# Eight of 22 up-projection steps as seven block products each, with the operand sums on GpSimd

## The chip, the cores and the metric

One Trainium2 chip, one of its cores. The metric is the device time of one execution in microseconds; the time of a kernel is the median of its runs.

## The reference, cut to what matters

One layer of a diffusion backbone over 512 latent tokens of width 1024, with 256 context tokens. A token mixer (a two-way state-space scan beside windowed attention) comes first. Its output is added to the stream, and then the part that the change touches follows, the gated feed-forward block:

```python
D_MODEL = 1024; SEQ = 512; D_FF = 2816

def conv_ffn(h, w_up, conv_w, conv_b, w_down):
    u = dwconv_centred(h @ w_up, conv_w, conv_b)     # 3 taps along the tokens
    a, b = u[..., :D_FF], u[..., D_FF:]
    return (jax.nn.silu(a) * b) @ w_down

x = x + gt1 * o_lat
x = x + gt2 * conv_ffn(modulate(x, norm2_g, sh2, sc2), w_up, ffn_conv_w, ffn_conv_b, w_down)
return rmsnorm(x, final_g)
```

All tensors are fp32.

## The kernel before

Every fp32 product is made as three products of a split operand. ScalarE rounds an operand to its high part (`hi`), VectorE subtracts to get the low part (`lo`), and TensorE adds up hi x hi, hi x lo and lo x hi in one PSUM bank. `split` (L180 to L182) does this for a piece of weights of 128 x 1024; `gemm` (L224 to L234) issues the matmuls, eight blocks of 128 of the inner dimension with three matmuls each, 512 tokens wide.

The program is a list of steps, each with the keys of the weights it needs. `run` walks the list and calls `load` for the weights one key ahead of the step that uses them; a load is a DMA on the SP queue into one of three `wraw` buffers and a split into one of two pairs of buffers `whi` and `wlo`. The order of each engine is then set by a scheduler that goes by readiness and by program order among what is ready. It is written out by hand only inside `manual_schedule`, and instructions given to `keep_in_program_order` keep their order among themselves.

The **up projection** has 22 steps (`up_step(t)`, NFF = 22). A step multiplies the normed input `h2h`, `h2l` (the high and low parts, tokens along the free dimension) with two weight pieces of 128 columns each: key `("up", t)` for the half called a, `("up", 22 + t)` for the half called b. Each half is one bank `pa` or `pb` of 512 tokens, 24 matmuls. `up_first` makes the convolution of a (a copy with scale on ScalarE, two multiply-adds on VectorE that read PSUM), a tanh, and the silu; `up_second` does the convolution of b and multiplies. The product goes to `F["x"][t % 2][:, t // 2]`. Step 0 is special: its matmuls are 256 wide, by halves of the tokens, since the input's norm is finished beside it (L1920). Eight pieces of the modulation vector (`m_step`, multiply-adds at L787 and L789) and eight transposes of the stream (`x1_turn`, L1950) are woven between the steps.

The **down projection** is already made as seven block products (`down_step(j, u)`, j = 0 to 6): the operand `F["x"]` is taken as four blocks, by the parity of t and by the halves of the tokens (`HALF`), called e, f, g and h in the code; the sums of weight blocks were formed in DRAM by accumulating DMAs, queued on GpSimd early in the program. The sums of operands are formed by `f_sums` at the end of each up step on VectorE, and `f_split` splits an operand of the next product into `F["s"]`, either there (for products 0 and 1) or during the product ahead. `near_last` and `near_out` finish the last rows after the last matmul.

There are eight PSUM banks, three under the name `acc` and five under `mis`. GpSimd does nothing in up steps 1 to 21.

## Time and profile before

| | us |
|---|---|
| median of 3 runs | 1225.29 |
| lowest and highest run | 1224.85, 1225.33 |
| the profiled execution, its own time | 1223.88 |
| its span | 1222.1 |
| TensorE busy | 1210.9 |
| VectorE busy | 919.6 |
| ScalarE busy | 682.7 |
| GpSimd busy | 196.2 |

The up projection lies at about 863 to 1107 us of the span and the down projection at 1107 to 1213. In the profile PE is TensorE's matmuls, PEld its weight loads, DVE is VectorE, ACT ScalarE, POOL GpSimd and SP the queue that issues most DMAs. A matmul's listed duration includes time in which the next one already runs, so busy PE time says only that it did not stop. A row of a group gives line, engine, operation, output and inputs, shapes and count, then busy time and mean duration in ns, then the engine's idle time just before and what ended it. A row of the timeline gives the start, the duration, and the instruction.

### The profile page before, as it was taken

How to read it: one execution, taken by the hardware profiler on the slowest of the kernel's cores; microseconds unless marked ns; L12 is line 12 of the kernel's file. 1: busy time of each engine (PE TensorE's matmuls, PEld its weight loads, DVE VectorE, ACT ScalarE, POOL GpSimd, SP SyncE). 2: the span in 40 equal slices, each digit the busy share in tenths (PEclk: the TensorE clock that was granted, in tenths of full speed). 3: DMA queues.
4: the chain of work that ended last, by engine and by line, in shares of the span. 5: the costliest groups of instructions: out<-in, count | busy, mean ns of one | idle time of the engine just before them, and what ended most of it. 6: DMA issues, size and time to landing. Idle time of an engine off the chain costs nothing.

```text
span 1222.1 us, 17422 instructions
## 1 busy us (share of the span) xinstructions
PE 1210.9 (99%) x6310; PEld 994.8 (81%) x6310; DVE 919.6 (75%) x1481; ACT 682.7 (56%) x1275; POOL 196.2 (16%) x187
## 2 busy tenths in 40 slices
PE   9999999999999999999999999999999999999996
PEld 6798888888878877778777778888988888888885
DVE  5857888888654598697896868577787777777786
ACT  5658788787444467486575663223543434335653
POOL 0000121101000043352451631000200000000053
PEclk9999999999999999999999999999999999999999
DMA  9645789844754435346365568777266533347852
GB/s 372 255 137 183 160 252 256 173 153 125 174 160 151 129 104 176 109 133 195 102 176 194 159 214 273 230 249 224 56 149 162 167 107 103 120 125 181 290 162 87
DMA packets 122551, 211.55 MB, mean 173 GB/s; under 512 B 26720, under 2 KB 69024, under 8 KB 122464
## 3 DMA queue, kind: packets, MB, share of 16 engines
q1 hardware_dynamic: 111280, 186.83, 48.8%
q0 software_dynamic: 10752, 23.07, 8.5%
q8 instruction: 50, 0.82, 0.3%
q10 hardware_dynamic: 432, 0.53, 0.1%
q14 instruction: 37, 0.30, 0.1%
HBM read 185.68 MB, written 42.28 MB: 187 GB/s over the span
## 4 chain that ended last, share of the span: by engine, by line
PE 95%; ACT 1%; DVE 1%; POOL 1%; issue 1%; DMA 0%; POOLq 0%; DVEq 0%; ACTq 0%
PE acc L231 20%; PE acc L234 20%; PE acc L232 20%; PE score L951 3%; PE po L1000 3%; PE pt L987 2%; PE mis L573 2%; PE mis L1604 2%; PE mis L1497 2%; PE mis L2102 1%; PE mis L2100 1%; PE mis L2101 1%; PE mis L1612 1%; PE acc L1070 1%; PE acc L1072 1%; PE acc L1071 1%
## 5 line engine op out<-in xcount | busy, mean ns | idle before, releaser
L181 ACT CAST whi<-wraw 128x1024 fp32r<-128x1024 f32 (+1 forms) x115 | 120.3, 1047 | 157.4 <-PE acc L232 113.3
L231 PE MATMUL acc<-hlh,whi 128*128 128x512 f32 x472 | 194.1, 411 | 0.0
L182 DVE TENSOR_TENSOR wlo<-wraw,whi 128x1024 fp32r<-128x1024 f32 (+1 forms) x115 | 144.1, 1253 | 64.4 <-ACT whi L181 61.0
L232 PE MATMUL acc<-hll,whi 128*128 128x512 f32 x472 | 185.0, 392 | 0.0
L234 PE MATMUL acc<-hlh,wlo 128*128 128x512 f32 x472 | 185.0, 392 | 0.0
L231 PE MATMUL acc<-mh,whi 128*128 128x512 f32 x368 | 143.4, 390 | 0.0
L232 PE MATMUL acc<-ml,whi 128*128 128x512 f32 x368 | 143.2, 389 | 0.0
L234 PE MATMUL acc<-mh,wlo 128*128 128x512 f32 x368 | 143.2, 389 | 0.0
L234 PEld LDWEIGHTS acc<-hlh,wlo 128*128 128x128 f32 x472 | 88.6, 188 | 19.5
L231 PEld LDWEIGHTS acc<-hlh,whi 128*128 128x128 f32 x472 | 88.8, 188 | 17.9 <-issue 3.1
L232 PEld LDWEIGHTS acc<-hll,whi 128*128 128x128 f32 x472 | 88.9, 188 | 17.4 <-issue 2.4
L234 PEld LDWEIGHTS acc<-mh,wlo 128*128 128x128 f32 x368 | 69.1, 188 | 14.5
L231 PEld LDWEIGHTS acc<-mh,whi 128*128 128x128 f32 x368 | 69.1, 188 | 14.3
L232 PEld LDWEIGHTS acc<-ml,whi 128*128 128x128 f32 x368 | 69.1, 188 | 14.1
L1385 DVE SCALAR_TENSOR_TENSOR ta<-acc,half,ta 128x511 f32<-128x511 f32 (+1 forms) x66 | 43.9, 665 | 26.4 <-ACT ta L1384 26.0
L960 DVE CUSTOM_DVE_ANT_0 p<-score,winm,nsink 128x512 f32<-128x512 f32 (+1 forms) x64 | 51.9, 810 | 15.3 <-PE score L951 13.8
L1384 ACT ACTIVATE ta<-acc,half 128x512 f32<-128x512 f32 (+1 forms) x66 | 46.8, 709 | 22.8 <-PE acc L234 21.6
L967 ACT ACTIVATE p<-p,mneg 128x512 f32<-128x512 f32 (+1 forms) x64 | 49.7, 778 | 15.4 <-DVE mneg L960 14.8
L162 POOL DMA_DIRECT2D dsum<-wdn x24 | 25.4, 1143 | 193.0 <-DVE wlo L1084 171.7
L1499 POOL TENSOR_TENSOR st<-st,eT 128x512 f32<-128x512 f32 x24 | 29.7, 1239 | 165.4 <-ACT st L1516 152.0
L231 PE MATMUL acc<-hch,whi 128*128 128x256 f32 x176 | 54.7, 311 | 0.0
L995 DVE TENSOR_TENSOR ptl<-pt,pth 128x512 fp32r<-128x512 f32 x72 | 47.5, 685 | 8.5 <-ACT pth L991 7.9
(426 smaller groups left out, 2998.7 us busy)
## 6 DMA issues: line engine op xcount, KB each, us to landing
wraw<-wup SPq DMA_DIRECT2D x44, 512.0 KB, 3.6
dsum<-wdn POOLq DMA_DIRECT2D x24, 704.0 KB, 9.0
fb<-cs_d SPq DMA_DIRECT2D x32, 512.0 KB, 6.3
wraw<-wm SPq DMA_DIRECT2D x32, 512.0 KB, 3.7
wraw<-wx SPq DMA_DIRECT2D x24, 512.0 KB, 3.5
wm<-wm SPq DMA_DIRECT2D x16, 512.0 KB, 8.0
wraw<-wz SPq DMA_DIRECT2D x16, 512.0 KB, 3.6
wraw<-wos SPq DMA_DIRECT2D x16, 512.0 KB, 4.6
```

The costliest lines, as they stand in the source:

```text
L181: S.copy(hi[:, :n], r[:, :n])
L182: return V.tensor_tensor(lo[:, :n], r[:, :n], raw(hi[:, :n]), ALU.subtract)
L231: T.matmul(ps, wh, xh[:, k0 + k, :], start=a, stop=False)
L232: T.matmul(ps, wh, xl[:, k0 + k, :], start=False, stop=False)
L234: T.matmul(ps, wl, xh[:, k0 + k, :], start=False, stop=b)
L951: T.matmul(ps[:, o : o + len(z) * P], Q[h][:, b * P : (b + 1) * P], k[:, j, z[0] * P : (z[-1] + 1) * P], start=v == 0 and o % 512 in (0, P ...
L960: V.tensor_tensor_reduce(p[:, :w], d["ps"][i][:, o0 : o0 + w], m, op0=ALU.add, op1=ALU.min, scale=1.0, scalar=nsink[:, h : h + 1], accum_o ...
L967: S.activation(p, p, AF.Exp, bias=d["mneg"][:, i : i + 1], scale=-1.0, accum_out=d["den"][:, i : i + 1])
L995: V.tensor_tensor(d["ptl"][x], d["pt"][x], raw(d["pth"][x]), ALU.subtract)
L1000: T.matmul(d["po"], vst[:, cols[x], j, :], d[y][x], start=x == 0 and y == "pth", stop=x == c - 1 and y == "ptl")
L1384: S.activation(o[:, :n], ps[:, :n], AF.Identity, scale=hcol(base_w, stride + i), bias=hcol(base_b, i))
L1385: V.scalar_tensor_tensor(o[:, 1:n], ps[:, 0 : n - 1], hcol(base_w, i), o[:, 1:n], ALU.mult, ALU.add)
```

## The change

Steps 5, 7, ... 19 of the up projection (`W_STEPS`) are made by `w_step` in place of `up_step`. The two weight pieces of a step (a above b, each with two halves of 512 of the inner dimension) and the input (two halves of the inner dimension, two of the tokens) are taken as 2 x 2 blocks, and the result is formed from seven products of blocks in place of eight. A product has four blocks of the inner dimension with three matmuls each, 256 tokens wide (`w_product`).

- Of the seven weight operands three are blocks as they are (two in `uA`, one in `uD`) and four are sums. `w_prepare`, called two steps ahead, loads the pieces with three DMAs and makes the sums with four 512-wide operations on GpSimd. `w_split` splits the sums into `F["wx"]`, two before the new step (in the ordinary step ahead of it) and two in it; `uA` and `uD` are split by `load` into the usual buffers.
- Four sums of input blocks are made once, in steps 0 to 2 (`h_work`, `h_sum`), on VectorE and GpSimd, and split into `F["hs"]`.
- In a new step three products are copied from PSUM by ScalarE, GpSimd adds three times 256 columns, and VectorE makes four 256-wide sums that write PSUM. Then the old `up_first` and `up_second` follow. The product of a and b is made on GpSimd in these steps.
- The operand sums of the down projection are no longer made in the up steps by VectorE (`f_sums` is gone) but in products 0 to 2 by GpSimd (`f_sum`). One operand is split with a changed sign. Product 1's operand is split during product 0. The operand tiles take the space of the new step's tiles once step 19 is over.
- The finish of the last rows changes its order: `near_last` is called by halves, and the roots come after.
- `x1_turn` uses another temporary, and the transposes and the row loads stand four places earlier among the steps.
- GpSimd's instructions of this whole last part of the program keep program order.

```diff
@@ load
+        if key[0] in ("uA", "uD"):
+            hi, lo = (wpool.tile([P, 1024], F32R, tag=x, name=x, bufs=2) for x in ("whi", "wlo"))
+            r = F["wr"][:, :1024] if key[0] == "uA" else F["wr"][:, 1024:]
+            split(r, r.shape[-1], hi, lo)
+            return hi, lo
@@ close_c1, up_second
-    def f_sums(t):
-        p, (x, y) = t // 2, F["x"]
-        e, f, g, h = (a[:, p, z] for a in (x, y) for z in HALF)
-        one = slice(p, p + 1)
-        if t % 2 == 0:
-            f_split(0, one, x[:, one, HALF[0]])
-            V.tensor_tensor(e, e, f, ALU.subtract)
-            f_split(1, one, x[:, one, HALF[0]])
+    FS = [slice(3 * i, min(3 * i + 3, DK)) for i in range(4)]
+    def f_sum(j, z):
+        e, f, g, h = (F["x"][i][:, z, HALF[u]] for i in range(2) for u in range(2))
+        t = F["t"][:, z, :]
+        if j == 1:
+            G.tensor_tensor(t, e, f, ALU.subtract)
+        elif j == 2:
+            G.tensor_tensor(t, t, h, ALU.add)
+        elif j == 4:
+            G.tensor_tensor(f, h, f, ALU.subtract)
+        else:
+            G.tensor_tensor(t, t, g, ALU.subtract)
...
-        V.tensor_tensor(F["x"][t % 2][:, t // 2, :], a, b, ALU.mult)
-        f_sums(t)
+        (G if t in W_STEPS else V).tensor_tensor(F["x"][t % 2][:, t // 2, :], a, b, ALU.mult)
...
+    W_STEPS = range(5, 20, 2)
+    def h_sum(i, u=None):
+        (eh, el), (fh, fl), (gh, gl), (hh, hl) = ([raw(x) for x in h_parts(i)] for i in range(4))
+        x, z = F["wr"][:, :1024].rearrange("p (k t) -> p k t", k=4), slice(0, 4)
+        if i == 0:
+            V.tensor_tensor(x, fh, eh, ALU.subtract)
+            V.tensor_tensor(x, x, fl, ALU.add)
+            V.tensor_tensor(x, x, el, ALU.subtract)
+        elif i == 2:
+            x, z = tmp("te").rearrange("p (k t) -> p k t", k=2), slice(2 * u, 2 * u + 2)
+            G.tensor_tensor(x, hh[:, z], fh[:, z], ALU.subtract)
...
+    def h_work(t):
+        if t == 0:
+            h_split(0, h_sum(0))
+            F["h"] = [h_sum(2, 0), h_sum(1), h_sum(2, 1)]
+        elif t == 1:
+            h_split(1, F["h"][1])
+            h_split(2, F["h"][0])
+            F["h"].append(h_sum(3))
+        elif t == 2:
+            h_split(3, F["h"][3])
+            h_split(2, F["h"][2])
...
+    def w_prepare(t):
...
+        nc.sync.dma_start(wr[:, :1024], top)
+        nc.sync.dma_start(s[0], low[:, :512])
+        nc.sync.dma_start(wr[:, 1024:], low[:, 512:])
...
+        G.tensor_tensor(s[2], a, s[0], ALU.subtract)
+        G.tensor_tensor(s[0], s[0], d, ALU.add)
+        G.tensor_tensor(s[1], s[0], a, ALU.subtract)
+        G.tensor_tensor(s[3], b, s[1], ALU.subtract)
+    def w_split(i):
+        hi, lo = (F["wx"][:, i, u, :] for u in range(2))
+        for u, r in enumerate((F["ws"][1 + i], F["ws"][3 * i])):
+            z = slice(512 * u, 512 * u + 512)
+            pin(S.copy(hi[:, z], r), V.tensor_tensor(lo[:, z], r, raw(hi[:, z]), ALU.subtract))
+    def w_step(t):
+        def fn(wa, wd):
+            b1, b3, b2, b5, b4 = accb(), accb(), misb(), misb(), misb()
+            w_split(1)
...
+            w_product(b1, wa, 0, e, True)
+            S.copy(p1, b1[:, :HL])
+            w_product(b2, wb, 0, t2, True)
+            S.copy(p6, b2[:, :HL])
+            G.tensor_tensor(p6, p1, p6, ALU.add)
+            w_product(b3, wd, 0, t4, True)
+            w_product(b1, wa, 1, g, False)
...
+            V.tensor_tensor(x, b3[:, :HL], p6, ALU.add)
+            w_product(b5, wc, 0, t3, True)
+            V.tensor_tensor(b3[:, :HL], b5[:, :HL], x, ALU.add)
+            w_product(b4, wb, 1, t1, True)
+            S.copy(p5, b4[:, :HL])
+            G.tensor_tensor(p1, p1, p5, ALU.add)
+            G.tensor_tensor(p5, p6, p5, ALU.add)
+            w_product(b2, wc, 1, h, False)
+            V.tensor_tensor(b1[:, HL:], b2[:, :HL], p1, ALU.add)
+            V.tensor_tensor(b3[:, HL:], b5[:, :HL], p5, ALU.add)
+            if t + 2 in W_STEPS:
+                w_prepare(t + 2)
+            a = up_first(b1, b3, t)
+            up_second(a, b3, t)
+        return [("uA", t), ("uD", t)], fn
@@ up_step
                 a = up_first(pa, pb, t)
+                if t + 1 in W_STEPS:
+                    w_split(0)
                 gemm([(pb, h2h, h2l)], wb)
             up_second(a, pb, t)
+            if t < 3:
+                h_work(t)
+            elif t == 20:
+                operand_tiles()
+            if t + 2 in W_STEPS:
+                w_prepare(t + 2)
+            if t > 19:
+                f_split(0, slice(0, 6) if t == 20 else slice(6, DK), F["x"][0][:, slice(0, 6) if t == 20 else slice(6, DK), HALF[0]])
@@ x1_turn
-            t = tmp("te")
+            t = hpool.tile([P, L], F32, tag="q2", name="xo")
@@ down_step
-                    for f in (near_last, near_out):
-                        for i in TWO:
-                            f(i)
+                    near_last(0, 0), near_last(0, 1)
+                    near_last(1, 0), near_root(0), near_last(1, 1), near_root(1)
+                    near_out(0), near_out(1)
...
+            if j == 0 and u == 0:
+                for z in FS:
+                    f_sum(1, z)
+            v = u - (j < 2)
+            if j < 6 and 0 <= v < 4:
+                z = FS[v]
+                f_split((j + 1) % 2, z, OPERAND[j + 1]()[:, z, :], j == 1)
+                if j in (0, 1, 2):
+                    f_sum((2, 6, 4)[j], z)
@@ the list of steps
-        + weave(weave([up_step(t) for t in range(NFF)], msteps[24:]), [([], lambda: None)] * 6 + [x1_turn(c) for c in range(8)] + [x1_rows] + [([], lambda: None)] * 7)
+        + weave(weave([(w_step if t in W_STEPS else up_step)(t) for t in range(NFF)], msteps[24:]), [([], lambda: None)] * 2 + [x1_turn(c) for c in range(8)] + [x1_rows] + [([], lambda: None)] * 11)
...
+    with tc.manual_schedule(engines={mybir.EngineType.Pool}):
+        run(prog, early=("g", 15))
```

More of the change, by code (lines that the diff above doesn't have):

```diff
@@ new lines, in w_split, with w_product @@
+    def w_split(i):
[3 more added lines that the diff above has]
+            pin(S.copy(hi[:, z], r), V.tensor_tensor(lo[:, z], r, raw(hi[:, z]), ALU.subtract))
+    def w_product(bank, w, u, x, first):
+        (wh, wl), (xh, xl) = w, x
+        with tc.manual_schedule(engines={mybir.EngineType.PE}):
+            for k in range(4):
+                c = slice(512 * u + k * P, 512 * u + k * P + P)
+                T.matmul(bank[:, :HL], wh[:, c], xh[:, k, :], start=first and k == 0, stop=False, skip_group_check=True)
+                T.matmul(bank[:, :HL], wh[:, c], xl[:, k, :], start=False, stop=False, skip_group_check=True)
+                T.matmul(bank[:, :HL], wl[:, c], xh[:, k, :], start=False, stop=k == 3, skip_group_check=True)
```

80 lines of the change are left out of this document (56 added, 24 removed).

## The prediction

> **What bounds the kernel now.** I read the page's head, its clock row and its chain of waits first.
>
> ```profile
> span 1222.1 us, 17422 instructions
> PE 1210.9 (99%) x6310; PEld 994.8 (81%) x6310; DVE 919.6 (75%) x1481; ACT 682.7 (56%) x1275; POOL 196.2 (16%) x187
> PEclk9999999999999999999999999999999999999999
> PE 95%; ACT 1%; DVE 1%; POOL 1%; issue 1%; DMA 0%; POOLq 0%; DVEq 0%; ACTq 0%
> ```
>
> TensorE carries 95% of the chain at an undiminished clock, so only fewer or shorter matmuls can gain, and any wait put into the matmul stream is paid in full. Then busy times by stretch: steps 1 to 21 of the up projection, one crowded stretch of the scan for comparison, and the first block of the down projection.
>
> ```profile
> 877.90:1107.00 229.10, 229.10 (x1017) 189.69 (x1016) 178.58 (x258) 94.89 (x130) 0.00 (x0) 1.00 0.44 131
> 600.00:640.00 40.00, 40.00 (x245) 31.39 (x244) 37.43 (x55) 31.46 (x79) 22.71 (x21) 1.00 0.55 164
> 1107.00:1122.00 15.00, 15.00 (x69) 12.41 (x68) 10.68 (x16) 7.58 (x10) 0.00 (x0) 1.00 0.99 187
> ```
>
> The columns are length, then PE, PEld, DVE, ACT, POOL, clock, DMA. In the 229.1 us of the 21 steps TensorE never stops, VectorE works 178.58, ScalarE 94.89 and GpSimd nothing.
>
> A listed matmul duration includes pipelining, so the price of one is the distance between starts, from the timeline: 512 columns wide in the up projection, then 256 columns wide just before it, with two weight loads of that stretch.
>
> ```profile
> 949.77 0.39 PE L231 MATMUL acc<-mh,whi 128*128 128x512 f32 x1
> ...
> 953.85 0.39 PE L231 MATMUL acc<-mh,whi 128*128 128x512 f32 x1
> ```
>
> ```profile
> 862.00 0.28 PE L1775 MATMUL acc<-mh,wlast 128*128 128x256 f32 x1
> ...
> 864.88 0.28 PE L1920 MATMUL acc<-ml,whi 128*128 128x256 f32 x1
> ```
>
> ```profile
> 862.12 0.19 PEld L1774 LDWEIGHTS acc<-ml,wlast 128*128 128x128 f32 x1
> 862.24 0.19 PEld L1775 LDWEIGHTS acc<-mh,wlast 128*128 128x128 f32 x1
> ```
>
> Eighteen spacings lie between the first two rows: 4.08 / 18 = 0.2267 us. Twenty-four between the next two: 2.88 / 24 = 0.120 us. The 0.19 us loads start every 0.12 us, so at 256 columns they still overlap.
>
> **TensorE's part.** A step has 2 x 8 x 3 = 48 matmuls of 512: 10.88 us. (21 of them make 228.5, and the stretch has 229.1.) A block-product step has 7 x 4 x 3 = 84 matmuls of 256: 10.08 us. Each of the eight replaced steps therefore saves 0.80, together **-6.4 us**. The margin is narrow: a spacing of 10.88 / 84 = 0.1295 would undo it. I take 0.120, because L1775 and L1920 load a new weight for each matmul as the new products do.
>
> The Trainium skill speaks against this: "TensorE: Matmul & The Clock Gate", section Back-to-back issue gap, gives sustained spacings of about 81 ns at 128 columns and 131 ns at 512. A line between them puts 256 at 98 ns, an estimate from that page by which a new step would cost 84 x 98 = 8.2 us against 48 x 131 = 6.3, 1.9 more. The trace does not agree: 227 ns at 512 and 120 ns at 256, so here the spacing follows the columns.
>
> **VectorE's part.** Rows for what is added and removed:
>
> ```profile
> 1115.37 1.23 DVE L182 TENSOR_TENSOR wlo<-wraw,whi 128x1024 fp32r<-128x1024 f32 x1
> 1116.52 0.69 DVE L182 TENSOR_TENSOR wlo<-dnraw,whi 128x512 fp32r<-128x512 f32 x1
> L1881 DVE SCALAR_TENSOR_TENSOR fx<-fx,fx 128x256 f32<-128x256 f32 x11 | 4.7, 424 | 0.3
> L1902 DVE TENSOR_TENSOR fx<-ta,tc 128x512 f32<-128x512 f32 x22 | 15.2, 690 | 0.6
> L1852 DVE SCALAR_TENSOR_TENSOR tb<-x,a,mis 128x256 f32<-128x256 f32 x16 | 6.9, 475 | 1.7 <-PE mis L293 1.5
> L789 DVE SCALAR_TENSOR_TENSOR tm<-wraw,csil,tm 128x512 f32<-128x512 f32 x42 | 32.3, 769 | 5.4 <-DMA wraw<-wm 4.6
> L181 ACT CAST whi<-dnraw 128x512 fp32r<-128x512 f32 x4 | 2.5, 614 | 0.3 <-PE mis L2101 0.3
> ```
>
> Back to back, each starts about 0.09 before the one ahead ends (1115.37 to 1116.52 is 1.15): 1.15 for a 1024-wide split, 0.60 for 512, 0.33 for a sum of 256 columns in SBUF, 0.40 with a PSUM operand. Two steps, an ordinary one and a new one, now take 2 x 178.58 / 21 = 17.0 of 21.76 us. Removed: six operand splits and sums per pair (2.0) and the new step's product of a and b (0.6, to GpSimd). Added: the seven weight operands need a 1024-wide split and five of 512 (4.15) where there were two of 1024 (2.3), so +1.85; four PSUM sums, +1.6. New need: **17.85 of 20.96 us**. ScalarE goes from 2 x 94.89 / 21 = 9.0 to about 11.5 (three more 512 copies, three 256 copies), far from binding.
>
> **GpSimd's part, and the port.** It gets, per pair, four 512-wide weight sums and the product of a and b, and three 256-wide sums. The nearest rows:
>
> ```profile
> L1617 POOL TENSOR_TENSOR dx<-dx,te 128x512 f32<-128x512 f32 x16 | 25.1, 1566 | 1.1
> L1857 POOL TENSOR_TENSOR ml<-ta,mh 128x256 fp32r<-128x256 f32 x8 | 5.9, 735 | 11.9 <-ACT ta L1856 11.9
> ```
>
> That is 5 x 1.57 + 3 x 0.74 = 10.0 us per pair, beside 20.96, and its results are wanted about half a step later or more. GpSimd itself is no bound. But the crowded stretch shows what it does to VectorE:
>
> ```profile
> 617.37 1.30 POOL L1615 TENSOR_TENSOR dx<-dx,te 128x512 f32<-128x512 f32 x1 [3.91 <-DVE te L1606]
> 618.74 2.16 POOL L1617 TENSOR_TENSOR dx<-dx,te 128x512 f32<-128x512 f32 x1
> ```
>
> ```profile
> 605.53 1.79 DVE L1393 SCALAR_TENSOR_TENSOR CT<-tb,ta 128x512 f32<-128x512 f32 x1
> 617.53 2.21 DVE L182 TENSOR_TENSOR wlo<-wraw,whi 128x1024 fp32r<-128x1024 f32 x1
> 619.67 1.51 DVE L1393 SCALAR_TENSOR_TENSOR tc<-tb,ta 128x256 f32<-128x256 f32 x1
> 627.59 1.19 DVE L1393 SCALAR_TENSOR_TENSOR tc<-tb,ta 128x512 f32<-128x512 f32 x1 [0.40 <-ACT tb L1392]
> 632.72 1.21 DVE L1393 SCALAR_TENSOR_TENSOR tc<-tb,ta 128x256 f32<-128x256 f32 x1
> 634.06 1.57 DVE L789 SCALAR_TENSOR_TENSOR tm<-wraw,csil,tm 128x512 f32<-128x512 f32 x1
> L1393 DVE SCALAR_TENSOR_TENSOR tc<-tb,ta x36: 405/692/1519, 377.0 to 656.3; 128x256 f32<-128x256 f32 x20, 128x512 f32<-128x512 f32 x16
> ```
>
> They take turns. The split started at 617.53 lasts 2.21 instead of 1.23: it runs only once GpSimd's sum has ended at 618.67. GpSimd's next sum then waits for it, and the operation of 619.67 waits for that. All stretched rows read two SBUF operands; each lasts 0.5 to 1.1 above its usual (1.23; 0.69 and 0.41 from L1393; 0.77). The six add 1.10 + 0.98 + 1.10 + 0.50 + 0.80 + 0.80 = 5.3 us to VectorE, for 22.71 us of GpSimd: 0.23 per us. The Trainium skill says in "GPSIMD Engine Reference", section Key points, only that both share their SBUF interfaces and contend when VectorE reads two SBUF inputs; the turns are the trace's. At 0.23, the new pair adds 2.3: **20.2 of 20.96**. The stretch at 600 has VectorE at 37.43 of 40 with TensorE unbroken, so 96% need not cost anything.
>
> What costs is the tightest deadline. In a new step the 512-wide operand "uD" takes the weight buffer freed when the step before ends, and is wanted by product three: its low part at 2 x 1.44 + 0.24 = 3.12 us after the start. Copy 0.61 and split 0.69 leave 1.8 of cover. Steps 9, 11 and 17 follow directly on a piece of the modulation, two multiply-adds (1.5), and with one stretch of 0.8 these exceed the cover by 0.5 each: 1.5; I add 0.1 for each of the other five. **+2.0 us**, between 0 (an order that puts that split first) and 6.4 (0.8 in each step). Other covers are longer: the next ordinary step's first weights are free at 5.76 and wanted at 10.08, against 2.3 of copy and split; the bank its second half needs is wanted 5.4 us after the new step, and freed by a sum, a copy and two additions in about 3.
>
> **Start of the stage.** Four sums of the input are made once, in steps 0 to 2.
>
> ```profile
> 876.10 0.71 DVE L1950 STREAM_TRANSPOSE te<-x 128x512 f32<-128x512 f32 x1
> 878.57 0.75 DVE L1385 SCALAR_TENSOR_TENSOR ta<-acc,half,ta 128x511 f32<-128x511 f32 x1 [1.76 <-ACT ta L1384]
> 881.22 1.22 DVE L182 TENSOR_TENSOR wlo<-wraw,whi 128x1024 fp32r<-128x1024 f32 x1
> ```
>
> The first sum is three 1024-wide subtractions (3 x 1.15). One fits the gap of 1.76; two come ahead of the split that now runs at 881.22 to 882.44, whose low part step 1 wants at 877.9 + 5.44 + 0.45 = 883.8. Cover 1.4, need 2.3 and a stretch of 0.3: **+1.2 us**, between 0 (split first) and 3.3 (none in the gap, one full stretch of 1.1). Later input sums have steps 1 to 4 to land. At this place the new operations pinned to program order queue VectorE and ScalarE behind GpSimd; with its 1024-wide sums at about 3 us (twice L1617) I price none, with 3 as the upper end.
>
> **Last stage.** GpSimd makes four times 11 x 256 = 2816 columns of sums (5.5 x 1.57 = 8.6 per block of 15 us). Block 0 gains four VectorE splits (3.4) and loses three sums (1.0).
>
> ```profile
> 1121.18 1.23 DVE L182 TENSOR_TENSOR dnw<-wraw,dnw 128x1024 fp32r<-128x1024 f32 x1 [3.98 <-ACT dnw L181]
> ```
>
> The idle 3.98 before this row hides it: 3.4 - 1.0 + 0.23 x 8.6 = 4.4, 0.4 over, which the block's last two parts, without such splits, take up. Nothing; 2 if that cover is gone. In the tail two halves change places:
>
> ```profile
> 1212.53 0.39 PE L2102 MATMUL mis<-wlo,fs 128*128 128x512 f32 x1
> 1213.31 0.42 DVE L2070 TENSOR_TENSOR ta<-mis,rowssq 128x256 f32<-128x256 f32 x1
> ```
>
> The second rows' work can start at 1212.92 instead of 1213.31: **-0.3**. GpSimd in program order and the DMAs moved on SP (three loads of the same bytes instead of two, transposed rows four places earlier) cost nothing: the stretch has DMA at 0.44, and GpSimd's operations there are the ones counted.
>
> **Sum.** -6.4 - 0.3 + 2.0 + 1.2 = -3.5. The profiled execution took 1223.88, 1.8 around its span; the median of the runs is 1.4 above it. I put the change on the median: 1225.29 - 3.5 = **1221.8 us**.
>
> **Rivals.** (1) The port makes VectorE the bound, slower than before. Price: VectorE's need per pair reaches 20.96 when the stretch is (20.96 - 17.85) / 10.0 = 0.31 per us of GpSimd; beyond that each 0.1 costs 1.0 per pair. Two-operand work is denser here than at 600 us, which speaks for it; GpSimd's sums are mostly wanted late and half of VectorE's work (convolutions, PSUM sums) reads one SBUF operand, which speaks against. At twice the ratio, 0.46: 22.45, 1.5 over, eight times 12; 1225.3 - 6.7 + 1.2 + 12 = 1232. (2) The fixed orders at the start and the input sums eat the gain: 3.3 + 3 there instead of 1.2, 1227, or with a bit less 1225, no difference. (3) The change does not do what it says: 256-wide matmuls across changing PSUM banks do not keep 0.120. At 0.135, eight steps cost 3.7 more than before: 1232. The rows with L1920 alternate banks, so this is unlikely. The spacings of the Trainium skill's page on TensorE, named above, would point this way. (4) All covers hold: -6.7, 1218.6, with up to a microsecond more where step 0 loses its three transposes.
>
> **How the numbers follow.** A measurement of this kernel tells about 0.2% (2.45 us) from no change. Forecast with rival 4, 1217 to 1222.8: 0.54. Between 1222.8 and 1227.7 (rival 2 and a forecast gone 2 us wrong): 0.18. Slower: rival 1 0.20, rival 2's far end 0.05, rival 3 0.03: 0.28. The range reaches from 1217.0 (all covers hold, and step 0 gains) to 1233.0 (rival 1 at twice the ratio); the likeliest cases alone span 1217.0 to 1224.0.
>
> **What would show it.** Right: 256-wide matmuls 0.120 apart in steps 5, 7, ... 19; a pair of steps in 21 to 21.5 us; VectorE two-operand rows stretched to 1.5 to 2.2 there; waits of TensorE on "wlo" of the 512-wide split, under a microsecond. Wrong: TensorE waiting on "wx" or "wlo" more than 0.8 per new step (rival 1), VectorE above 97% of the pairs; or waits on input sums in steps 1 to 5 (rival 2); or a spacing above 0.13 without a wait (rival 3).

## The result, and the profile after

| | before | after |
|---|---|---|
| median, us | 1225.36 (6 runs) | 1260.82 (6 runs, 1258.57 to 1262.31) |
| ratio | | 1.0285, 95% interval 1.0272 to 1.0299 |
| the profiled execution | 1223.88 | 1260.52 |
| its span | 1222.1 | 1258.7 |

The change makes the kernel 35.5 us slower; the forecast was 3.5 us faster, with 1233 as its upper end. The head, the clock row and the chain's shares of the page after:

```profile
span 1258.7 us, 18221 instructions
PE 1221.8 (97%) x6598; PEld 1010.9 (80%) x6598; DVE 961.2 (76%) x1485; ACT 706.6 (56%) x1320; POOL 337.5 (27%) x277
PEclk9999999999999999999999999999899999998999
PE 8%; DVE 6%; POOL 2%; issue 2%; DMA 1%; ACT 1%; POOLq 0%; DVEq 0%; ACTq 0%
```

Two things differ. The chain is no longer TensorE's (95% before, 8% now), and the clock row has two slices at 8. GpSimd's busy time rose by 141 us, VectorE's by only 42. VectorE is still a quarter idle in the mean, so the mean doesn't say where the time is. Busy times by stretch do (columns: length, PE, PEld, DVE, ACT, POOL, clock, DMA):

```profile
878.00:900.00 22.00, 17.68 (x78) 13.90 (x77) 19.43 (x20) 8.37 (x13) 17.00 (x10) 0.84 0.24 59
933.00:1106.00 173.00, 162.19 (x1001) 144.47 (x1000) 138.29 (x191) 80.37 (x129) 69.19 (x58) 0.99 0.40 124
1106.00:1133.00 27.00, 24.10 (x99) 19.10 (x99) 21.92 (x24) 12.55 (x16) 11.74 (x8) 0.94 0.29 85
1133.00:1180.00 47.00, 39.57 (x161) 30.88 (x160) 40.27 (x32) 24.80 (x31) 29.33 (x12) 0.93 0.73 193
```

TensorE stops in each of them, for the largest share of the time in the first and the last, which hold no new step at all. From the starts of the first and last matmuls of the stages in both traces:

| stage | before, us | after, us | difference |
|---|---|---|---|
| steps 0 to 4 (input sums) | 57.7 | 67.5 | +9.9 |
| steps 5 to 19 (eight of them new) | 163.7 | 174.6 | +10.9 |
| steps 20, 21 | 22.1 | 27.2 | +5.1 |
| down projection to its last matmul | 105.5 | 116.8 | +11.3 |
| after the last matmul | 9.6 | 8.7 | -0.9 |

With 0.4 ahead of step 0 this is, but for rounding, the 36.6 by which the spans differ. TensorE's own need in steps 5 to 19 is 8 x 10.08 + 7 x 10.88 = 156.8, so 17.8 us are lost there, of which the saving of matmuls pays back 6.4 (0.5 was lost there before as well).

**Steps 1 and 2.** GpSimd's rows (the input sums), VectorE's, then TensorE's:

```profile
888.07 2.73 POOL L1957 TENSOR_TENSOR wr<-mh,wr 128x1024 f32<-128x1024 f32 x1 [2.46 <-DVE hs L1940]
890.88 3.22 POOL L1958 TENSOR_TENSOR wr<-wr,ml 128x1024 f32<-128x1024 f32 x1
```

```profile
888.50 3.37 DVE L182 TENSOR_TENSOR wlo<-wraw,whi 128x1024 fp32r<-128x1024 f32 x1
891.80 2.85 DVE L1920 TENSOR_TENSOR fx<-ta,tc 128x512 f32<-128x512 f32 x1
```

```profile
888.50 0.40 PE L237 MATMUL acc<-ml,whi 128*128 128x512 f32 x1
891.93 0.79 PE L239 MATMUL acc<-mh,wlo 128*128 128x512 f32 x1 [3.04 <-DVE wlo L182]
892.52 0.63 PE L236 MATMUL acc<-mh,whi 128*128 128x512 f32 x1
892.95 0.63 PE L237 MATMUL acc<-ml,whi 128*128 128x512 f32 x1
```

The split that takes 1.22 alone takes 3.37: it ends 1.07 after GpSimd's sum, about one undisturbed split. The next VectorE operation does the same with the next sum (2.85 instead of 0.69). TensorE stands for 3.04, and then its matmuls start 0.43 apart instead of 0.227, ten of them, before the spacing comes back: the granted clock is 0.84 in the stretch from 878 to 900. So a long wait was paid more than in full, by about 2 us.

**A new step.** The pair of steps from product two of step 15 to product two of step 17:

```profile
1053.01:1075.59 22.58, 21.66 (x132) 19.22 (x132) 18.91 (x26) 10.63 (x18) 9.57 (x8) 1.00 0.36 118
```

```profile
1070.05 1.73 POOL L1920 TENSOR_TENSOR fx<-ta,tc 128x512 f32<-128x512 f32 x1 [0.63 <-DVE ta L1911]
```

```profile
1070.55 2.31 DVE L182 TENSOR_TENSOR wlo<-wr,whi 128x1024 fp32r<-128x1024 f32 x1
...
1075.67 1.29 DVE L1992 TENSOR_TENSOR wx<-te,wx 128x512 fp32r<-128x512 f32 x2
```

```profile
1074.47 0.28 PE L1999 MATMUL acc<-mh,whi 128*128 128x256 f32 x1
1074.59 0.28 PE L2000 MATMUL acc<-ml,whi 128*128 128x256 f32 x1
1074.71 0.28 PE L2001 MATMUL acc<-mh,wlo 128*128 128x256 f32 x1
1075.59 0.39 PE L1999 MATMUL mis<-hs,wx 128*128 128x256 f32 x1 [0.60 <-ACT wx L1992]
```

The new matmuls do start 0.120 apart, and VectorE is busy 18.91 of 22.58, 84%: neither the spacing nor VectorE's load is the bound. The split of `uA` (1070.55) meets GpSimd's product of a and b and takes 2.31; convolution, tanh and silu queue behind it; and the first two weight sums are split behind those (1075.67), when product two already waits. In the last pair the split came just ahead of that product (1091.97, 1.21 us long), the product on GpSimd took 2.21 instead of 1.28, and product two waited for nothing.

**Down projection.** One VectorE row for each of four GpSimd sums (three of 768 columns, the last of 512):

```profile
1166.96 9.54 POOL L1902 TENSOR_TENSOR fx<-fx,fx 128x768 f32<-128x768 f32 x4
```

```profile
1167.47 2.60 DVE L1889 TENSOR_TENSOR fs<-fx,fs 128x768 fp32r<-128x768 f32 x1
1169.99 2.86 DVE L182 TENSOR_TENSOR wlo<-wraw,whi 128x1024 fp32r<-128x1024 f32 x1
1172.78 2.59 DVE L1889 TENSOR_TENSOR fs<-fx,fs 128x768 fp32r<-128x768 f32 x1
1175.29 2.29 DVE L182 TENSOR_TENSOR wlo<-dnraw,whi 128x1024 fp32r<-128x1024 f32 x1
```

TensorE waits 1.6 and 1.7 here. At the stage's start, where three sums in a row (1132.13 to 1139.69) meet the split of the first weights, it waits 4.1 and then runs eleven matmuls 0.43 apart. In the step before, ScalarE stands 4.65 for an operand sum ahead of a tanh; in the rest of that step TensorE waits only 0.25:

```profile
1120.23 0.84 ACT L1888 CAST fs<-ft 128x768 fp32r<-128x768 f32 x1 [4.65 <-POOL ft L1898]
```

The one long wait of steps 20 and 21 (with slow matmuls behind it) comes earlier, ahead of the first operand sum at 1117.89. VectorE first waits for GpSimd's last addition of step 19, then for a piece of the modulation, and TensorE waits for its convolution:

```profile
1106.93 0.43 DVE L2030 TENSOR_TENSOR acc<-mis,te 128x256 f32<-128x256 f32 x1 [2.46 <-POOL te L2027]
1109.80 0.75 DVE L794 SCALAR_TENSOR_TENSOR tm<-wraw,csil,tm 128x512 f32<-128x512 f32 x1 [2.10 <-DMA wraw<-wm]
1114.33 0.47 PE L236 MATMUL acc<-mh,whi 128*128 128x512 f32 x1 [2.65 <-DVE ta L1391]
```

### The profile page after: what moved, and what is told of

Same layout as the page of the kernel before. It is cut to its first block, busy times and chain, and to the rows that moved or that the text cites. A ratio compares the mean times of both kernels' runs of the same rounds, so it can differ in the third digit from the quotient of the medians.

```text
span 1258.7 us, 18221 instructions
## 1 busy us (share of the span) xinstructions
PE 1221.8 (97%) x6598; PEld 1010.9 (80%) x6598; DVE 961.2 (76%) x1485; ACT 706.6 (56%) x1320; POOL 337.5 (27%) x277
## 5 line engine op out<-in xcount | busy, mean ns | idle before, releaser
L181 ACT CAST whi<-wraw 128x1024 fp32r<-128x1024 f32 (+1 forms) x99 | 103.5, 1045 | 129.5 <-PE acc L237 52.5
L182 DVE TENSOR_TENSOR wlo<-wraw,whi 128x1024 fp32r<-128x1024 f32 (+1 forms) x99 | 133.2, 1347 | 46.0 <-ACT whi L181 43.0
L236 PE MATMUL acc<-mh,whi 128*128 128x512 f32 x240 | 96.0, 400 | 7.5 <-ACT whi L181 4.3
L239 PE MATMUL acc<-mh,wlo 128*128 128x512 f32 x240 | 95.0, 397 | 3.3 <-DVE wlo L182 3.3
L237 PE MATMUL acc<-ml,whi 128*128 128x512 f32 x240 | 95.2, 397 | 0.0
L1504 POOL TENSOR_TENSOR st<-st,eT 128x512 f32<-128x512 f32 x24 | 30.1, 1255 | 165.0 <-ACT st L1521 151.9
L236 PEld LDWEIGHTS acc<-mh,whi 128*128 128x128 f32 x240 | 46.0, 192 | 19.1 <-ACT whi L181 5.8
L972 ACT ACTIVATE p<-p,mneg 128x512 f32<-128x512 f32 (+1 forms) x64 | 49.9, 779 | 15.3 <-DVE mneg L965 14.8
L239 PEld LDWEIGHTS acc<-mh,wlo 128*128 128x128 f32 x240 | 46.0, 192 | 13.8 <-DVE wlo L182 4.1
L794 DVE SCALAR_TENSOR_TENSOR tm<-wraw,csil,tm 128x512 f32<-128x512 f32 x56 | 45.8, 817 | 14.2 <-DMA wraw<-wm 13.6
```

Source lines behind the costliest of these rows:

```text
L181: S.copy(hi[:, :n], r[:, :n])
L182: return V.tensor_tensor(lo[:, :n], r[:, :n], raw(hi[:, :n]), ALU.subtract)
L236: T.matmul(ps, wh, xh[:, k0 + k, :], start=a, stop=False)
L237: T.matmul(ps, wh, xl[:, k0 + k, :], start=False, stop=False)
L239: T.matmul(ps, wl, xh[:, k0 + k, :], start=False, stop=b)
L794: V.scalar_tensor_tensor(acc, r[:, u * 512 : u * 512 + 512], sc, acc, ALU.mult, ALU.add)
```

## The experiments

Theory: GpSimd's sums hold VectorE operations that TensorE needs at once, in all stages, and the orders in the new steps do the rest. Rivals: the new steps alone; the orders alone; GpSimd's time in all and not the width of one sum. Differences are against the kernel before, run on the same chip (1225.1 to 1226.4), or, where it says so, against the 1260.82 of after. A kernel without an interval behind its time ran once, and executions of the kernel before range from 1223.9 to 1229.7, so the stages of each trace are read beside the times.

### What each part costs

**The operand sums of the last stage, the order of GpSimd and the new tail, without the new steps and input sums.**

```diff
-    W_STEPS = range(5, 20, 2)
+    W_STEPS = ()
-            if t < 3:
-                h_work(t)
-            elif t == 20:
+            if t == 20:
```

> The changed kernel with all 22 up steps ordinary and no input sums; only the operand sums of the last stage stay on GpSimd. Theory (the operand sums cost by themselves: wide GpSimd sums hold the shared port, and the queues of ScalarE and VectorE wait behind them): steps 20 and 21 and the down projection lose the 16 us that they lose in the changed kernel, so about 1241. Rival (the last stage only suffers because step 19 ends late and with VectorE in arrears): 1226 to 1229.

Measured 1234.41, +8.7. Between the two. VectorE operations are stretched here as well (by some 12 us in all for 22.4 us of GpSimd from 1107 to 1155), with waits of TensorE of 1.4 at step 0 and 1.5, 1.4 and 1.6 in the down projection, and slow matmuls behind the first and the third of these. Steps 20 and 21 lose nothing.

**After, without the operand sums.** The calls of `f_sum` go, and products take operands as they are.

```diff
-                for z in FS:
-                    f_sum(1, z)
+                pass
-                if j in (0, 1, 2):
-                    f_sum((2, 6, 4)[j], z)
```

> The changed kernel without the operand sums of the last stage: the splits take unsummed blocks. Theory (the sums themselves cost): 16 us less than the changed kernel, about 1245. Rival (arrears from the new steps): 1256 to 1260.

Measured 1254.52, 6.3 below after: less than half of the stages' losses. Steps 20 and 21 still lose 4.0 us, which come from the new steps (the table below). The down projection still loses 6.1. Its one long wait of TensorE (3.4, slow matmuls behind it) is for a copy whose weights landed late; why they did stays open:

```profile
1149.99 1.04 ACT L181 CAST dnw<-wraw 128x1024 fp32r<-128x1024 f32 x1 [8.46 <-DMA wraw<-dsum]
```

**After, without the input sums** (`h_work` splits the blocks as they are).

> The changed kernel without the four input sums: the four splits in steps 0 to 2 take unsummed blocks. Theory (the 1024-wide GpSimd sums in steps 1 and 2 hold VectorE's splits): 8 to 9 us of the 11 lost before step 5 come back, about 1252; some 2 stay, from GpSimd's fixed order in step 0. Rival (the first VectorE sum and the four splits crowd VectorE): only 3 us, 1257.

Measured 1253.21, 7.6 below after, as the theory said. (The three subtractions on VectorE are left out with them, so the run alone doesn't tell them from GpSimd's; the rows of steps 1 and 2 do.)

**After, without GpSimd's work in the new steps**: weight sums and the additions of products are left out, and the product of a and b is back on VectorE.

```diff
-        G.tensor_tensor(s[2], a, s[0], ALU.subtract)
...
-            G.tensor_tensor(p6, p1, p6, ALU.add)
...
-        (G if t in W_STEPS else V).tensor_tensor(F["x"][t % 2][:, t // 2, :], a, b, ALU.mult)
+        V.tensor_tensor(F["x"][t % 2][:, t // 2, :], a, b, ALU.mult)
```

> The changed kernel without any GpSimd work in the new steps: the splits take unsummed weights, the three additions are left out, and the product of a and b is on VectorE. Theory (GpSimd holds the port when the split of uA comes, and the splits of the weight sums queue behind it): the new steps fall to their 10.1 us and the kernel to 1246 to 1249. Rival (the order on ScalarE and VectorE is late by itself, since the splits of the weight sums stand behind the tanh and the silu of the step ahead): at most 5 us come back, 1256 or more.

Measured 1245.48, 15.3 below after: the theory. TensorE's waits on `wx` (2.2 and 2.2 us from 930 to 1110 in after) are gone; its waits on the copy `whi` and the split `wlo` of the new steps, 3.1 and 1.9, stay.

**None of GpSimd's sums** (the three edits above together).

> The changed kernel with none of its sums on GpSimd (weight sums, three additions, input sums, operand sums, product of a and b on VectorE); all matmuls, splits, loads and PSUM sums stay. Theory (GpSimd's sums and what queues behind them are the whole loss): the 256-wide products give their 6.4 us, less about 2.5 for GpSimd's order in step 0 and 1 to 2 of late splits: 1221 to 1224. Rival (the additional splits and PSUM sums crowd VectorE in any case): 1230 or more.

Measured 1227.91, 1.8 above before. Two things follow. The sums, all on GpSimd but the first input sum, cost 1260.8 - 1227.9 = 33 of the 35 us. And without any of them the 6.4 us of TensorE are gone all the same:

```profile
PE acc L236 <- ACT whi L181: 3.1, 3, 1.1
PE acc L1996 <- DVE wlo L182: 1.9, 2, 1.0
PE acc L2039 <- POOL ml L1862: 1.4, 1, 1.4
```

These are TensorE's three largest waits from the waits view of this run (total, times, longest). The last is at step 0, the others in the new steps.

The stages of these traces, in us, show which sums each loss goes with:

| kernel | steps 0 to 4 | 5 to 19 | 20, 21 | down projection |
|---|---|---|---|---|
| before | 57.7 | 163.7 | 22.1 | 105.5 |
| after | 67.5 | 174.6 | 27.2 | 116.8 |
| operand sums without new steps | 59.8 | 163.7 | 22.1 | 113.6 |
| after, no operand sums | 67.5 | 174.8 | 26.2 | 111.6 (late weights) |
| after, no input sums | 58.7 | 176.6 | 26.5 | 116.9 |
| after, no GpSimd in new steps | 65.9 | 165.1 | 22.3 | 117.1 |
| none of the sums | 59.8 | 165.0 | 22.1 | 106.7 |

The input sums account for most of the loss in steps 0 to 4, GpSimd's work in the new steps for most of it in steps 5 to 21, the operand sums for most of it in the down projection.

### Orders

**Before, with GpSimd's program order only.** A `manual_schedule` of GpSimd around the last part.

> The kernel before with nothing changed but GpSimd's instructions of the last part in program order. Theory (in step 0 three low parts of the input queue on GpSimd behind a root that waits for TensorE): a wait of about 1.5 us in step 0 and half-speed matmuls behind it, 2 to 3 us slower, 1228. Rival (order on an idle GpSimd is free, as predicted): within 0.5 us of the kernel before.

Measured 1227.24, +1.2: between the two. The trace is with the theory: steps 0 to 4 take 60.1 instead of 57.7, with a wait of 1.8, and the other stages are as before. GpSimd's low parts of the input now stand behind the root, which waits for TensorE and VectorE:

```profile
867.68 0.70 POOL L287 TENSOR_TENSOR rs<-ms,phalf 128x2 f32<-128x2 f32 x1 [4.76 <-DVE ms L286]
868.34 3.31 POOL L1857 TENSOR_TENSOR ml<-ta,mh 128x256 fp32r<-128x256 f32 x3
```

**After, with the split of the first two weight sums ahead.**

```diff
+                if t + 1 in W_STEPS:
+                    w_split(0)
                 gemm([(pa, h2h, h2l)], wa)
                 a = up_first(pa, pb, t)
-                if t + 1 in W_STEPS:
-                    w_split(0)
```

> The changed kernel with the split of the first two weight sums placed ahead of the first product of the ordinary step before a new step, so that it no longer stands behind that step's convolution, tanh and silu. Theory (the order of ScalarE and VectorE makes these splits late, by GpSimd's hold of about 1.1 us): TensorE's wait in product two (0.9 + 0.5 in most new steps) goes, 6 to 10 us less, about 1252. Rival (the GpSimd sums themselves are late): the split now waits for GpSimd in order and holds the ordinary step's splits, 1260 or slower.

Measured 1257.42, 3.4 below after. Between: product two hardly waits now, but product three, whose operand is split next, does.

**After, with the up steps' matmuls under `manual_schedule`.**

> The changed kernel with the matmuls of the ordinary up steps kept in program order with those of the new steps. Theory (the scheduler drew two 512-wide matmuls of the next step in between products three and four of steps 7, 9 and 11; their weights take the buffer of uD, which product three only then frees, so TensorE stands 1.2 to 1.3 us for a copy on ScalarE): these three waits go, 3 to 5 us less, about 1256. Rival (these waits only move to the next late split): within 1 us of the changed kernel.

Measured 1260.9, no change. The edit did not do what it was for: in the trace two matmuls of the next step still stand between products and wait 1.2, three times. It keeps each half step together, not behind the step ahead; so this run tells nothing about that order (the last one below does).

**Before, with the new tail order.**

> The kernel before with the new order of the last rows alone. Theory (the second rows start when their matmul is done, not behind the first rows' root): 0.3 to 0.9 us less, 1224.5 to 1225.1. Rival (the chain after the last matmul is the same): no difference.

Measured 1225.47 against 1225.23, ratio 1.0001 (0.9988 to 1.0015): no difference. The 0.3 us forecast for it can't be told from nothing. In the trace the stretch behind the last matmul is 9.4 us against 9.6, so the order doesn't explain the 0.9 of the table above either.

**None of the sums, and three orders together**: split ahead, half steps together, GpSimd in program order only after step 0.

> None of GpSimd's sums (weight, product, operand and input sums are left out, so these operands hold other numbers), and besides three orders are changed: the split of the first two weight sums stands ahead of the step before's convolution, the up steps' matmuls run as written, and GpSimd keeps its written order only after step 0. The theory that the 9 us which ate the 6.4 us without any sums (1227.91 against 1226.07) are orders: the waits of that run were 1.53 at step 0, 1.22 and twice 1.18 before matmuls that were pulled in between products, and twice 1.1 for the late split; all go but some of the last, so about 1226.1 + 1.8 - 6 = 1220 to 1222. Rival, that the steps' buffers and copies set these waits whatever the order: 1225 or more.

Measured 1223.67, ratio 0.9986 (0.9976 to 0.9996). So orders are part of it: 1.6 us of gain come out, 3.5 better than the single run without them; in the traces steps 0 to 4 gain 2.4 (57.3) and steps 5 to 19 another 2.4 (162.6). The three waits for `whi` remain.

**The same, with the matmuls tied to the written order.**

```diff
+                if a and "hs" in F:
+                    tc.keep_in_program_order(m0)
...
+                if k == 3:
+                    tc.keep_in_program_order(m0)
```

> As e13 (none of GpSimd's sums, split first), and now the matmuls of an ordinary step really stand behind those of the new step ahead of it: the last matmul of each block product and the first of each half step keep program order. In e13 two matmuls of the next step still ran between products and waited 1.2 three times for a weight copy. The theory that this is what is left of the lost gain: 1223.7 - 3.5 = 1220 to 1221. Rival, that the copy is late anyway and the wait only moves to the start of the next step or to another operand: 1223 to 1224.

Measured 1227.05 against 1226.44, ratio 1.0003 (0.9992 to 1.0015): the rival. The matmuls now stand as written, and the wait has gone over to the next product of the same steps:

```profile
946.54 1.04 ACT L181 CAST whi<-wraw 128x1024 fp32r<-128x1024 f32 x1 [2.90 <-PE acc L1997]
947.49 1.14 ACT L1989 CAST wx<-wr 128x512 fp32r<-128x512 f32 x2
```

```profile
946.34 0.28 PE L1998 MATMUL acc<-hs,wlo 128*128 128x256 f32 x1
948.15 0.39 PE L1996 MATMUL mis<-hs,wx 128*128 128x256 f32 x1 [1.54 <-ACT wx L1989]
```

ScalarE's order puts the copy into a weight buffer that TensorE still reads ahead of the copies of `wx`, and both wait for the end of product three. So an order on ScalarE holds the largest waits that are left; another one there wasn't tried, and steps 5 to 19 lose 8.3 us here, of which these three waits are 5.1. (In the profiled execution a late transfer cost the down projection 3.5 us besides, and slow matmuls behind it.)

### The width of a sum

**After, with the wide sums in pieces of 256 columns** (input sums L1957, L1958 and operand sums).

```diff
-            G.tensor_tensor(x, a, x, ALU.subtract)
+            for k in range(4):
+                G.tensor_tensor(x[:, k], a[:, k], x[:, k], ALU.subtract)
```

> The changed kernel with the wide GpSimd sums (1024 columns in the input sums, 768 and 512 in the operand sums) cut into pieces of 256 columns. Theory (what hurts is how long one GpSimd sum holds the port: 2.7 to 3.2 us before a split that takes 1.2): VectorE's split waits one piece of 0.74 at a time, the added time per GpSimd us falls from about 0.5 to 0.2 in these stages, 10 us less, about 1250. Rival (what counts is GpSimd's total and the waits for its results): no change, 1258 to 1263.

Measured 1253.37, 7.5 below after. VectorE's stretch from 886 to 933 (what its rows last above their usual) falls from 10.7 to about 7.5 us, though GpSimd works longer there (30.2 instead of 23.6), and the split beside an input sum takes 1.76 instead of 3.37. The down projection gains 4.2, although this execution too has weights that landed late there (TensorE waits 3.1 for them), so narrow sums may be worth more than the time shows.

**Narrow sums, split ahead, half steps together, GpSimd's order after step 0.**

> The changed kernel with four things together: narrow pieces of the sums, the first two weight sums split ahead of the step, matmuls of the up steps in program order, and GpSimd's program order only after step 0. Theory (the losses are separate): 7.5 + 3.4 + 4 + 1.5 less than the changed kernel, about 1244, still slower than the kernel before. Rival (they cover each other): 1250 or more.

Measured 1252.55: hardly better than narrow sums alone. In steps 20 and 21 ScalarE now waits 10.2 us in three times for GpSimd's operand sums, and TensorE's longest wait of the run, 4.3 at step 20, ends with a copy behind one of them.

**Before, with sums on GpSimd that nobody reads**: in steps 2 to 11 one of 1024 columns behind the product of a and one behind that of a and b, in steps 12 to 21 four of 256 in these places.

```diff
+        for i in range(1 if t < 12 else 4):
+            g = G.tensor_tensor(o, x, y, ALU.add)
+            if i == 0:
+                tc.add_manual_dep(g.ins, ins.ins.name, BEHIND, reason="beside a step")
...
+        if t > 1:
+            idle_sums(t, ins)
```

> The kernel before with idle sums on GpSimd whose results nobody reads: in steps 2 to 11 two of 1024 columns per step, in steps 12 to 21 eight of 256, half behind the silu and half behind the product of a and b. Theory (the port alone stretches VectorE, and wide sums more than narrow ones): VectorE gains about 0.45 per GpSimd us in the first half and 0.2 in the second, TensorE waits for late splits in the first half alone, 1228 to 1233. Rival (only waits for GpSimd's results cost): no stretch that reaches TensorE, 1225 to 1227.

Measured 1265.67, +40.4: far more than either. This was the surprise: no new wait by data, no changed order of the steps, and GpSimd busy in them for some 136 us more. A pair of wide ones:

```profile
942.60 2.40 POOL L1879 TENSOR_TENSOR ft<-fs 128x1024 f32<-128x1024 f32 x1 [5.25 <-DVE ta L1908]
948.40 2.57 POOL L1879 TENSOR_TENSOR ft<-fs 128x1024 f32<-128x1024 f32 x1 [3.40 <-DVE fx L1919]
```

```profile
942.70 3.38 DVE L182 TENSOR_TENSOR wlo<-wraw,whi 128x1024 fp32r<-128x1024 f32 x1 [0.25 <-ACT whi L181]
...
948.63 2.62 DVE L1897 TENSOR_TENSOR fx<-fx,fx 128x256 f32<-128x256 f32 x1
```

Each sum adds 2.2 us to one VectorE operation, and TensorE then loses 0.9 to 2.8 to a wait for the split, in nearly every half step from 917 to 1036 us. So an ordinary step has about 1 us of slack for its split (2.2 less the usual loss of 1.0 to 1.5). Behind 1036 us, beside the narrow sums, there are two such waits.

**Only the wide ones, steps 2 to 11.**

> The same as the narrow one, in the same steps 2 to 11 and at the same places, but one sum of 1024 columns in the place of four of 256: 20 sums, about 49 us of GpSimd. Width theory: each holds one VectorE instruction for some 2.2 us, which is about 1.5 us more than the step can hide: 20 times 1.0 to 1.5, with slow matmuls behind the longest waits, 22 to 32 us over the kernel before, though GpSimd is busy for little more than half as long as in the narrow one. Rival, that the time of GpSimd counts and not the width: about half of what the narrow one costs.

Measured 1253.47, ratio 1.0228 (1.0213 to 1.0243), +28.2 with 48.8 us of GpSimd.

**Four of 256 in the same places, only the first of four tied there.**

> The kernel before with sums of 256 columns on GpSimd that nobody reads, in steps 2 to 11 only: four behind the product of a and four behind that of a and b, 80 in all, about 87 us of GpSimd. Width theory: a VectorE instruction waits out one GpSimd instruction at a time, 0.4 to 0.55 us for 256 columns; the split of 1.21 takes 1.7 instead of 3.4, most of which the slack of about 0.7 us takes up: 3 to 8 us over the kernel before. Rival, that GpSimd work of any width beside the split stops the step: as with the wide sums, 24 us or more.

Measured 1258.65, ratio 1.0274 (1.0259 to 1.0289), +33.3, which looks like the rival but isn't. The three untied ones of each four ran early, in rows, beside steps 0 to 3. They stood ahead of the input's low parts (TensorE waited 2.1 to 5.6 five times beside step 0), and held one split, for which TensorE waited 11.3, for a whole row of sums:

```profile
898.81 16.51 POOL L1877 TENSOR_TENSOR ft<-fs 128x256 f32<-128x256 f32 x24
```

```profile
902.80 13.61 DVE L182 TENSOR_TENSOR wlo<-wraw,whi 128x1024 fp32r<-128x1024 f32 x1
```

From 922 us to the end of the up projection, with one sum of 256 left at each place, TensorE didn't wait at all.

**All four tied**, each in columns of its own:

```diff
-            if i == 0:
+            if True:
                 tc.add_manual_dep(g.ins, ins.ins.name, BEHIND, reason="beside a step")
```

> The kernel before with idle sums of 256 columns on GpSimd in steps 2 to 11, now all four of each place tied behind the product of a, or of a and b, so that they run there and not early; the four touch different columns and follow each other without a pause. Width theory: VectorE waits out one of them at a time, the split of 1.21 takes about 1.7 to 2.2 and its neighbours 0.5 more each: 3 to 10 us over the kernel before. Rival, that a chain of sums without a pause holds VectorE as long as it lasts (the narrow run had one split of 13.61 beside 24 such sums in a row): 4 times 0.7 holds the split as long as one sum of 1024 does, and the cost is that of the wide ones, about 28 us.

Measured 1234.53, ratio 1.0076 (1.0061 to 1.0091): +9.4.

**All four tied, each adding to the result of the one before.**

> The same, but each of the four adds to the result of the one before, in the same 256 columns, so that GpSimd may pause between them. Width theory: as with the independent ones, 3 to 10 us over the kernel before. Rival, that it is pauses which let VectorE in: clearly cheaper than the independent ones, under 10 where those cost about 28.

Measured 1230.63, ratio 1.0044 (1.0027 to 1.0061): +5.5. The width theory holds: at the same places, with the same columns, one wide sum costs 28.2 in all and four narrow ones 5.5 to 9.4, although the narrow ones keep GpSimd busy for longer. The sums and the splits (those from 900 to 1000 us) by groups, first in the wide run, then in the run with four narrow ones in their own columns:

```profile
L1877 POOL TENSOR_TENSOR ft<-fs 128x1024 f32<-128x1024 f32 x20 | 48.8, 2438 | 106.6 <-DVE ta L1906 71.7 <-DVE fx L1917 34.9
L182 DVE TENSOR_TENSOR wlo<-wraw,whi 128x1024 fp32r<-128x1024 f32 x15 | 34.9, 2325 | 2.6 <-ACT whi L181 2.6
```

```profile
L1877 POOL TENSOR_TENSOR ft<-fs 128x256 f32<-128x256 f32 x80 | 78.5, 1012 | 60.8 <-DVE ta L1906 53.6 <-DVE fx L1917 7.3
L182 DVE TENSOR_TENSOR wlo<-wraw,whi 128x1024 fp32r<-128x1024 f32 x17 | 27.6, 1626 | 2.6 <-ACT whi L181 2.3 <-DMA x_d<-te 0.2
```

A split takes 2.33 in the mean beside wide sums, 1.63 beside narrow ones, and 1.22 in the kernel before:

```profile
L182 DVE TENSOR_TENSOR wlo<-wraw,whi 128x1024 fp32r<-128x1024 f32 x19 | 23.3, 1224 | 12.2 <-ACT whi L181 11.3 <-DMA x_d<-te 1.0
```

Whether pauses between sums let VectorE in, the rival of the last run, is not settled: 5.5 against 9.4 is cheaper, but not as clearly as it asked.

## Why the prediction was wrong

- **TensorE's part held.** 256-wide matmuls start 0.120 apart in every new step, and rival 3 is out.
- **The loads held.** GpSimd works 9.57 us per pair (10.0 forecast), VectorE 18.91 (20.2), and the stretch in steps 5 to 19 is some 12.3 us for 69.6 us of GpSimd, 0.18 per us (0.23). Rival 1, the port making VectorE the bound, needed 0.31 and full pairs: it is out as a mechanism, although its time was on the right side.
- **The step that failed is the treatment of the port as added load.** The stretch was summed over a pair (0.23 x 10.0 = 2.3) and compared with the pair's length. It arrives in lumps, one GpSimd instruction long, and a lump that meets a split with about 1 us of slack goes to TensorE. The price was set by width and place. The "tightest deadline" was sought at `uD`, with a cover of 1.8; the ordinary steps' own splits, which the argument took as covered, have less, about 1 us (the idle sums).
- **The W-step term of +2.0** (0 to 6.4) was mis-sized: 17.8 us are lost in steps 5 to 19. Over the spacing, the expected gaps at `uD` are there, 1.6 and 1.4 in steps 9 and 11 and 0.3 in step 13. To them come 1.2 in three steps (7, 9 and 11) for the copy of the next weights, and at product two 1.0 to 1.4 in five of the eight (7, 9, 13, 15 and 17), for weight sums split behind the silu. The other 5 are shorter waits and slower matmuls. "Wanted about half a step later or more" was true of GpSimd's results, not of the splits behind them.
- **The start term of +1.2** (0 to 3.3, and 3 for the pinned order) was +9.9. The order of GpSimd, priced at none, cost about 2.5 by itself in that stage. The later input sums "have steps 1 to 4 to land", which they do; what they hold meanwhile was not priced. GpSimd's 1024-wide sums had been put at 3 us, which is right (2.73 and 3.22).
- **The last stage, priced at nothing, "2 if that cover is gone",** cost 11.3 in the down projection. (The 5.1 of the two steps ahead go with GpSimd's work in the new steps: they are gone without it and stay without the operand sums.) The idle 3.98 before one VectorE row is no cover for the first weights' split at the start of the stage. The ratio of 0.23 was read beside 512-wide sums; beside sums of 768 and more columns it is about 0.45 (886 to 933) to 0.52 (1133 to 1180). And ScalarE, priced as far from binding, was held in order for the operand sums, though TensorE waited only 0.25 in the rest of that step.
- **"Paid in full" was too little.** Three waits of 2.7 us and more each brought ten or so matmuls at 0.43 instead of 0.227, some 6 us in all.
- **The tail's -0.3** can't be told from nothing. The signs named as wrong did come: waits on `wx` and `wlo` above 0.8 in six of the eight new steps, and waits in steps 1 to 5 (for a split held by an input sum, not for the sum itself); VectorE above 97% did not.

None of the kernels that do all of the work is faster than the kernel before. Without any of GpSimd's sums, and with better orders, 1.6 us were gained.

## What to carry to other kernels

Before moving work to GpSimd, list the VectorE operations with two SBUF operands that another engine waits for, and their slack: one GpSimd operation may delay one of them by nearly its whole length, so what counts is the length of a single instruction against that slack, not the load of either engine. If work must go there, cut it into pieces shorter than the slack and tie each piece to a place; pieces that are free to run early gather in rows. A saving of half a per cent on the bounding engine is worth nothing until the orders of the engines that feed it have been checked too, since each copy and split that moves by a microsecond takes its share back.

## What the runs showed of the hardware

- A VectorE operation with two SBUF operands waits for the end of a GpSimd sum: 1.22 became 3.38 beside a sum of 2.40. The Trainium skill, page "SBUF — State Buffer", section "SBUF: two separate sides", says that whichever of the two engines starts first has the shared ports for its whole instruction while the other blocks; the rows agree, and the other way round too: a split that started first made GpSimd's product take 2.21 instead of 1.28. A look at that rule instead of a ratio would have given the lumps.
- Beyond one instruction: beside 24 sums of 256 columns in a row (16.51 us) one split lasted 13.61. Beside rows of four, and of eight in the run with both kinds, it lasted at most 1.76. What decides whether VectorE gets in between two sums stays open.
- Behind each of the three longest waits of TensorE in after (2.7, 3.0 and 4.1 us) its matmuls came 0.43 apart for seven to eleven matmuls, and the granted clock is 0.50 there (from 889.9 to 896.7, 1115.2 to 1118.5 and 1139.1 to 1145.8). Behind the two of 1.6 and 1.7 in the down projection it stayed at 1.00; but it fell to 0.50 behind one of 1.4 in step 0 (869.4 to 872.8), and in step 9 behind waits of 1.4 and 1.0 in a row (985.5 to 988.8, matmuls of 256 columns 0.213 apart). "TensorE: Matmul & The Clock Gate" in the Trainium skill, section "Part 1: The HAM clock gate", has the clock fall after an idle window of about 3.4 us whose start runs freely; that fits the length of the slow stretches, about 3.4 or 6.8 us, better than the cases behind short waits.
